# Class 3's routing ahead of class 2's gates, and the first 32 tiles multiplied in SBUF

## The chip, the cores and the metric

The kernel runs on one core of a Trainium2 chip. TensorE (PE) multiplies matrices, VectorE (DVE) and ScalarE (ACT) work element by element, GpSimd (POOL) issues the gathers, SyncE (SP) issues the plain loads and stores. The metric is the device time of one execution in microseconds.

## The reference

One encoder block for 512 tokens of width 1024, in float32. The token-mixing half ends in a residual `x`. The channel-mixing half, which this case is about, is a product-key retrieval layer:

```
h = rmsnorm(x) ;  q = (h @ w_q) in 8 heads x 2 halves of 128
s = q . sub_keys                    # 128 scores for each head and half
top_s, top_i = top_k(s, 16)         # 16 of 128, each half
best_s, best_j = top_k(all 256 sums of a pair, 16)
expert = i0 * 128 + i1 ;  gate = softmax(best_s)     # 8 x 16 = 128 of 16384 experts a token
act = gelu(u_tab[expert] . h) * gate
x = x + sum(act * v_tab[expert]) ;  out = rmsnorm(x)
```

`u_tab` and `v_tab` are 16384 x 1024 each, 67 MB each.

## The kernel before

The 512 tokens are four classes of 128 (class r holds the tokens t with t mod 4 = r). Classes 0 and 3 are *gathered*: for each of a token's 128 experts one row of `u` and one of `v` is fetched by an indirect DMA (`row_of`, L237, 128 rows of 4 KB for 128 tokens, 0.52 MB), and DVE multiplies and sums (L261, L344). Classes 1 and 2 (`ND` = 2, together 256 columns, `TD`) are done *densely*: all 16384 experts, in 128 tiles of 128, are multiplied on PE, and a dense matrix of gates, zero but for the 128 chosen experts of each token, is multiplied in.

**Order.** Class 0's front half comes first, exactly, then that of classes 1 to 3 together. Meanwhile class 0's gathers run as `steps` (L118): a generator that yields after each gathered row. `gather_steps` (L124) is called at fixed places of the stream of work, adds an estimated duration times `rate`, and takes that many steps; so the gathers are spread by estimates, not by need. Class 0 has 256 steps (`NA`), class 3 has 261 (`NCL`): four of routing, 128 rows of `u`, 128 of `v` and the end. By the code some 215 of the 517 are taken before the early tiles; each early tile takes 4.5 x 0.38 = 1.71. The rest is spread evenly over the main loop (L811).

**Routing** (`route`, L175) is DVE work only: the two top-16 searches and the pick of the expert numbers for two heads; four calls make a class. Classes 1 and 2 are routed at L696 to L710, in the pool `l2`. Class 3's scores go to DRAM (`s_dram`, L712) and come back in `gathered` (L322), which is class 3's generator, at L327 to L332: it routes, casts the numbers to `eidx` (L335), and goes on to the rows.

**Gates** (`gates`, L748) of class r: PE transposes expert numbers and gates; DVE writes two one-hots for eight tokens at a time (`hot`, L768), ACT scales one of them (L771), PE multiplies them to gates of 128 x 128 experts for each token (`pg`, L776), ACT copies these to `stg` (L779), and one DMA for each 32 tokens writes `stg` to `g_dram` (L780). Both classes' gates are issued by L797 to L804 with the same priority, class 1's, then class 2's routing, then class 2's gates.

**Early tiles** (`early`, L784). For 28 pairs of tiles the up-projection is done ahead: tiles of `ut` are loaded (0.52 MB each, four buffers `rawp`), multiplied in plain float32 by `h2T` (L742, `mm`), and go through gelu (L743). The first 20 pairs stay in SBUF (`KEPT`, the tile `pre`), the other eight go to DRAM (`SPILLED`, `a_dram`). `G0` and `G1` hold two of the pairs behind the transposes of class 1's and class 2's gates on PE.

**Main loop** (L827). Every 8 tiles two loads bring the gates of both classes (`gl`, L831). For a pair of tiles the activations are there (kept), loaded (spilled), or computed (`up_pair` with `h2S`, split in two float32r halves, three products). Then the activations are multiplied by the gates (L849), split, and multiplied with the split tile of `v` into `acc` (L861). At the end `finish` (L221) normalises and writes.

SP, DVE, ACT, PE and POOL each work through one list in order; the lists are laid out when the kernel is built, by priorities and estimated durations.

Of the kernel before, what the change touches and what calls it, by code (L numbers as in the profile page):

```python
# [9 lines left out]
F32 = mybir.dt.float32  # L10
# [4 lines left out]
ALU = mybir.AluOpType  # L15
# [4 lines left out]
P = 128  # L20
# [8 lines left out]
NC = 50  # L29
ND = 2  # L30
TD = ND * P
NB = 4 * ND

NPRE = 40
NSP = 16
KEPT = list(range(0, NPRE, 2))
SPILLED = list(range(NPRE, NPRE + NSP, 2))

# [1 line left out]
GB = 16  # L40
# [9 lines left out]
VUS = 2.75  # L50

G0 = 3
G1 = 12
LATE = 15.0


def body(ctx, tc, a, out):
    nc = tc.nc
# [63 lines left out]
    taken = 0  # L122
# [120 lines left out]
    def in_row(name, k, n):  # L243
        row = gp.tile([P, D], F32, tag="row", name=name, bufs=GPB)
        return row[:, 0:k * n].rearrange("p (k n) -> p k n", k=k)
# [4 lines left out]
    def routed():  # L250
        return [gp.tile([P, 8, 16], F32, tag=t, name=t + "_g") for t in ("bv", "ef")]
# [70 lines left out]
    def gathered(r, behind):  # L322

        h2g = gp.tile([P, D], F32, tag="h2g", name="h2g")
        nc.sync.dma_start(h2g, h2_dram)
        bv, ef = routed()
        for c in range(4):  # L327
            sg = in_row("sg", 4, P)
            nc.sync.dma_start(sg, s_dram[c])
            for _ in route(gp, sg, bv[:, 2 * c:2 * c + 2, :], ef[:, 2 * c:2 * c + 2, :], row_eq):  # L330
                pass
            yield  # L332
        eidx = gp.tile([P, P], I32, tag="eidx", name="eidx")
        gate = gp.tile([P, P], F32, tag="gate", name="gate")
        nc.vector.tensor_copy(eidx, ef.rearrange("p h k -> p (h k)"))  # L335
        softmax16(bv, gate)
        xg = load_x(r)
        pend = []

        def down():  # L340
            k0, act = pend.pop(0)
            for k in range(GB):
                row = row_of(a["v"], eidx[:, k0 + k:k0 + k + 1])
                nc.vector.scalar_tensor_tensor(xg, row, act[:, k:k + 1], xg, op0=ALU.mult, op1=ALU.add)  # L344
                yield

        for k0 in range(0, P, GB):
            ab = gp.tile([P, GB], F32, tag="abk", name="ab", bufs=2)
            yield from u_rows(eidx, h2g, ab, k0, GB)
            if k0 == 0:  # L350
                behind()
            act = gp.tile([P, GB], F32, tag="act", name="act", bufs=3)
            nc.scalar.activation(act, ab, AF.Gelu)
            nc.vector.tensor_tensor(act, act, gate[:, k0:k0 + GB], ALU.mult)
            if pend:
                yield from down()
            pend.append((k0, act))
        yield from down()
        finish(gp, r, xg)
        yield  # L360


    NA, NCL = 256, 261
    gp = pool(ctx, "gp", 1, side="right", reuse_waits="tile")

    ph = ExitStack()
# [3 lines left out]
    with ExitStack() as p1:  # L370
# [317 lines left out]
        late = []  # L688
        gs_ = [l2.tile([P, P], F32, name=f"g{r}") for r in range(ND)]

        def gate_of(r):
            sums.append(softmax16(bvs[r], gs_[r]))
# [3 lines left out]
        def route_now(j, c, ssb):  # L696
            for _ in route(l2, ssb, bvs[j][:, 2 * c:2 * c + 2, :], efs[j][:, 2 * c:2 * c + 2, :],
                           lambda: l2.tile([P, 16, NC], F32, tag="eq", name="eq")):
                pass
# [48 lines left out]
    def gates(r, ef, g):  # L748
        e = l2.tile([P, P], I32, tag="e", name="e", bufs=1)
        nc.vector.tensor_copy(e, ef.rearrange("p h k -> p (h k)"))  # L750
        ij = l2.tile([P, 2, P], I32, tag="ij", name="ij", bufs=1)
        nc.vector.tensor_scalar(ij[:, 0, :], e, 7, None, op0=ALU.logical_shift_right)
        nc.vector.tensor_scalar(ij[:, 1, :], e, 127, None, op0=ALU.bitwise_and)
        ijf = l2.tile([P, 2, P], F32, tag="ijf", name="ijf", bufs=1)
        nc.vector.tensor_copy(ijf, ij)
        t = ppg.tile([P, 4, P], F32, tag="pg", name="tr")
        for k, src in enumerate((ijf[:, 0, :], ijf[:, 1, :], g)):
            tr = nc.tensor.transpose(t[:, k, :], src, ident)
        trs.append(tr)
        tt = l2.tile([P, 3, P], F32, tag="tt", name="tt")  # L760
        nc.scalar.copy(tt, t[:, 0:3, :])
        for blk in range(4):
            stg = gb.tile([P, P, 32], F32, tag="stg", name="stg")
            for b8 in range(4):
                c0 = blk * 32 + b8 * 8
                hot = [gb.tile([P, 8, P], F32, tag=f"hot{k}", name="hot") for k in range(2)]
                for k in range(2):
                    nc.vector.tensor_tensor(hot[k], iota.unsqueeze(1).to_broadcast([P, 8, P]),  # L768
                                            tt[:, k, c0:c0 + 8].unsqueeze(2).to_broadcast([P, 8, P]), ALU.is_equal)
                for m in range(8):  # L770
                    nc.scalar.activation(hot[0][:, m, :], hot[0][:, m, :], AF.Copy,  # L771
                                         scale=tt[:, 2, c0 + m:c0 + m + 1])
                for q in range(2):
                    ps = ppg.tile([P, 4, P], F32, tag="pg", name="pg")
                    for m in range(4):
                        nc.tensor.matmul(ps[:, m, :], hot[1][:, 4 * q + m, :], hot[0][:, 4 * q + m, :],  # L776
                                         start=True, stop=True)
                    c1 = b8 * 8 + 4 * q
                    nc.scalar.copy(stg[:, :, c1:c1 + 4].rearrange("p i c -> p c i"), ps)  # L779
            nc.sync.dma_start(g_dram[r][blk], stg)  # L780

    npre = len(KEPT) + len(SPILLED)
    rate = PRE
    def early(n, behind=None):  # L784
        i = (KEPT + SPILLED)[n]
        if n < len(KEPT):
            up_pair(i, lambda k: pre[:, 2 * n + k, :], PUS, behind=behind)
            return
        ges = [gep.tile([P, TD], F32, tag="ge", name="ges") for _ in range(2)]
        up_pair(i, lambda k: ges[k], PUS, behind=behind)  # L790
        for k in range(2):
            nc.sync.dma_start(a_dram[2 * (n - len(KEPT)) + k], ges[k])

    trs = []
    for n in range(G0):
        early(n)
    with tc.high_priority(offset=1500):  # L797
        for r in range(ND):
            gates(r, efs[r], gs_[r])
            if r == 0:  # L800
                with tc.issue_after(sums[0].ins):
                    for args in late:
                        route_now(*args)
                gate_of(1)  # L804
    for n in range(G0, npre):
        early(n, trs[0] if n == G0 else trs[1] if n == G1 else None)
    pr_.close()
    assert taken > NA + 5 + GB
    pva.close()
    pacc = pool(ctx, "pacc", 1, space=PSUM, reuse_waits="tile")  # L810
    rate = (NA + NCL - taken) / ((P - 2 * npre) * UUS + P * VUS - LATE)  # L811
# [15 lines left out]
    for i in range(0, P, 2):  # L827
        if i % 8 == 0:
            gl = glp.tile([P, NB, 8, 32], F32, tag="gl", name="gl")
            for r in range(ND):  # L830
                nc.sync.dma_start(gl[:, 4 * r:4 * r + 4, :, :],  # L831
                                  g_dram[r][:, :, i:i + 8, :].rearrange("b j i c -> j b i c"))
        if i in KEPT:
            ge = [pre[:, i + k, :] for k in range(2)]
        else:
            ge = [gep.tile([P, TD], F32, tag="ge", name="ge") for _ in range(2)]
            if i in SPILLED:
                for k in range(2):
                    nc.sync.dma_start(ge[k], a_dram[2 * SPILLED.index(i) + k])
            else:  # L840
                up_pair(i, lambda k: ge[k], UUS, h2S)
        ops = []
        for k in range(2):
            g3 = ge[k].rearrange("p (b c) -> p b c", c=32)
            raw = load(vt, i + k)
            vh = hip.tile([P, D], F32R, tag="hi", name="vh")
            vl = lop.tile([P, D], F32R, tag="lo", name="vl")
            split(vh, vl, raw)
            nc.vector.tensor_tensor(g3, g3, gl[:, :, (i + k) % 8, :], ALU.mult)  # L849
            ah = ep.tile([P, TD], F32R, tag="ah", name="ah")  # L850
            al = ep.tile([P, TD], F32R, tag="al", name="al")
            last = split(ah, al, ge[k])
            ops.append(([ah, al], [vh, vl]))
            gather_steps(VUS, last)
        order = [(k, t, q) for k in range(2) for t in range(ND) for q in range(2)]
        if i == P - 2:
            order = [(k, t, q) for t in range(ND) for q in range(2) for k in range(2)]
        for k, t, q in order:
            c = slice(t * P, t * P + P)
            f = slice(q * 512, q * 512 + 512)  # L860
            mm(acc[t][:, f], [x[:, c] for x in ops[k][0]], [x[:, f] for x in ops[k][1]], False, i + k == P - 1)  # L861
# [75 lines left out]
```

## Time and profile before

| | us |
|---|---|
| median of 3 runs (1809.59 to 1811.98) | 1809.87 |
| the profiled execution | 1802.23 |
| its span, first to last instruction | 1800.5 |
| PE busy | 1623.4 (90%) |
| DVE busy | 1324.7 (74%) |
| ACT busy | 714.4 (40%) |
| POOL busy | 691.9 (38%) |

548.53 MB were moved, 305 GB/s over the span. Early tiles begin at 813 us, the main loop's first tile of `v` is issued at 1116 us, and its first computed pair ends its up-projection at 1342 us.

The rows below come from several views of one profiled execution. Times are in us from the span's start, durations of one instruction in ns where marked. A busy time is the union of the instructions' spans, with their number behind it (x). The DMA share is the mean busy share of the core's 16 DMA engines. In square brackets stands the idle time of the engine before an instruction, and what ended it.

### The profile page before, as it was taken

Reading aid. Unit: us, or ns where it says so; the run is one execution under the profiler, and the core shown is the slowest. Engines: PE = TensorE matmul, PEld = TensorE weight load, DVE = VectorE, ACT = ScalarE, POOL = GpSimd, SP = SyncE. Lnnn points to the kernel's source line nnn. Section 1 sums busy time; section 2 is a strip of 40 time slices with the busy share of each in tenths; the row PEclk is TensorE's granted clock in tenths of the full one; section 3 lists DMA queues with packets and bytes.
Section 4 is the critical chain, followed back from the end, with each engine's and each line's share of the span. In section 5 each row is a group of like instructions: output and inputs, shape, how many; then the busy total and the mean of one; then the engine's idle time right before and its main releaser. Section 6 shows DMA issues by size and latency. Waiting matters only on the chain.

```text
span 1800.5 us, 25509 instructions
## 1 busy us (share of the span) xinstructions
PE 1623.4 (90%) x9184; PEld 1379.4 (77%) x9184; DVE 1324.7 (74%) x2818; ACT 714.4 (40%) x1264; POOL 691.9 (38%) x535
## 2 busy tenths in 40 slices
PE   7999987899689997999999967778989999999997
PEld 6988867777489874887878956556768887888886
DVE  3332119899999344589957966899989888888895
ACT  4324211344443323224777711233444443444443
POOL 0000000277776443333430044566545454444440
PEclk9999999898899998999999988799999999999999
DMA  5335776499999899777885599999999999999994
GB/s 198 94 108 154 262 259 212 159 366 354 315 331 355 308 358 363 272 292 265 306 318 203 213 392 401 362 396 380 363 392 373 354 380 356 374 365 358 372 353 148
DMA packets 164335, 548.53 MB, mean 305 GB/s; under 512 B 17008, under 2 KB 37488, under 8 KB 163056
## 3 DMA queue, kind: packets, MB, share of 16 engines
q1 hardware_dynamic: 90480, 278.43, 43.3%
q0 software_dynamic: 73728, 268.47, 39.6%
q8 instruction: 72, 1.18, 0.3%
q14 instruction: 55, 0.45, 0.1%
HBM read 522.19 MB, written 24.64 MB: 304 GB/s over the span
## 4 chain that ended last, share of the span: by engine, by line
PE 58%; DVE 20%; DMA 10%; issue 6%; ACT 4%; POOL 2%; DVEq 0%; SPq 0%; POOLq 0%; ACTq 0%
PE pj L112 7%; PE pj L114 6%; PE pj L116 6%; PE pj L115 6%; PE pu_t L112 5%; DVE row L261 5%; PE acc L115 5%; PE acc L116 4%; PE acc L114 4%; DMA raw<-in_ut_dram 4%; DVE vl L90 3%; PE acc_A L295 3%; DMA row<-in_u_dram,eidx 2%; PE pg L776 2%; PE pu_t L116 2%
## 5 line engine op out<-in xcount | busy, mean ns | idle before, releaser
L239 POOL DMA_INDIRECT row<-in_u_dram,eidx x256 | 357.0, 1394 | 407.5 <-DVE eidx L335 98.8
L261 DVE SCALAR_TENSOR_TENSOR row<-row,h2g 128x1024 f32<-128x1024 f32 x256 | 308.4, 1222 | 9.6 <-DMA row<-in_u_dram,eidx 9.3
L239 POOL DMA_INDIRECT row<-in_v_dram,eidx x128 | 181.2, 1415 | 169.8 <-DVE xg L344 82.5
L115 PE MATMUL acc<-vl,ah 128*128 128x512 f32 x512 | 208.3, 416 | 33.7 <-DVE vl L90 33.5
L239 POOL DMA_INDIRECT row<-in_v_dram,eT x128 | 143.9, 1125 | 223.9 <-PE acc_A L295 175.8
L112 PE MATMUL pu_t<-h2T,raw 128*128 128x256 f32 x896 | 207.6, 388 | 21.7 <-DMA raw<-in_ut_dram 21.7
L112 PEld LDWEIGHTS pu_t<-h2T,raw 128*128 128x128 f32 x896 | 171.0, 195 | 53.6 <-issue 26.2
L114 PE MATMUL acc<-vh,ah 128*128 128x512 f32 x512 | 192.1, 408 | 17.4 <-ACT vh L89 15.4
L90 DVE TENSOR_TENSOR wlo<-raw,whi 128x1024 fp32r<-128x1024 f32 x88 | 107.7, 1223 | 130.3 <-ACT whi L89 130.3
L116 PE MATMUL acc<-vh,al 128*128 128x512 f32 x512 | 199.5, 406 | 0.3 <-DVE al L90 0.3
L89 ACT CAST whi<-raw 128x1024 fp32r<-128x1024 f32 x88 | 92.1, 1048 | 248.3 <-PE pj L115 174.4
L90 DVE TENSOR_TENSOR vl<-raw,vh 128x1024 fp32r<-128x1024 f32 x128 | 155.6, 1222 | 23.8 <-ACT vh L89 23.5
L114 PE MATMUL pu_t<-h2S_hi,uhi 128*128 128x256 f32 x576 | 165.0, 286 | 5.6 <-ACT uhi L89 4.5
L116 PE MATMUL pu_t<-h2S_hi,ulo 128*128 128x256 f32 x576 | 165.1, 287 | 3.9 <-DVE ulo L90 3.8
L344 DVE SCALAR_TENSOR_TENSOR xg<-row,act,xg 128x1024 f32<-128x1024 f32 x128 | 164.1, 1282 | 0.6
L115 PE MATMUL pu_t<-h2S_lo,uhi 128*128 128x256 f32 x576 | 164.3, 285 | 0.0
L115 PEld LDWEIGHTS acc<-vl,ah 128*128 128x128 f32 x512 | 99.9, 195 | 72.9 <-DVE vl L90 52.4
L89 ACT CAST vh<-raw 128x1024 fp32r<-128x1024 f32 x128 | 133.0, 1045 | 31.5 <-DMA raw<-in_v_dram 21.8
L114 PEld LDWEIGHTS acc<-vh,ah 128*128 128x128 f32 x512 | 96.6, 195 | 44.9 <-ACT vh L89 22.7
L151 POOL TENSOR_TENSOR rs<-ms,mhalf 128x1 f32<-128x1 f32 x16 | 9.0, 562 | 298.8 <-DVE ms L149 298.7
L114 PEld LDWEIGHTS pu_t<-h2S_hi,uhi 128*128 128x128 f32 x576 | 111.3, 193 | 10.8 <-ACT uhi L89 7.2
L116 PE MATMUL pj<-hT_hi,wlo 128*128 128x384 f32 (+1 forms) x320 | 101.1, 356 | 19.5 <-DVE wlo L90 19.5
(241 smaller groups left out, 3387.7 us busy)
## 6 DMA issues: line engine op xcount, KB each, us to landing
raw<-in_ut_dram SPq DMA_DIRECT2D x128, 512.0 KB, 6.7
raw<-in_v_dram SPq DMA_DIRECT2D x128, 512.0 KB, 6.6
raw<-in_w_in_dram SPq DMA_DIRECT2D x88, 512.0 KB, 4.4
raw<-in_wq_dram SPq DMA_DIRECT2D x32, 512.0 KB, 4.5
g_dram<-stg SPq DMA_DIRECT2D x8, 2048.0 KB, 7.8
gl<-g_dram SPq DMA_DIRECT2D x32, 512.0 KB, 9.3
raw<-in_wa_dram SPq DMA_DIRECT2D x16, 512.0 KB, 6.1
raw<-in_wo_dram SPq DMA_DIRECT2D x16, 512.0 KB, 4.8
```

What stands on the lines that cost most here:

```text
L89: nc.scalar.copy(hi, src)
L90: return nc.vector.tensor_tensor(lo, src, hi.bitcast(F32), ALU.subtract)
L112: on_pe = nc.tensor.matmul(ps, l[0], r[0], start=first, stop=last)
L114: nc.tensor.matmul(ps, l[0], r[0], start=first, stop=False)
L115: nc.tensor.matmul(ps, l[0], r[1], start=False, stop=False)
L116: on_pe = nc.tensor.matmul(ps, l[1], r[0], start=False, stop=last)
L151: nc.gpsimd.tensor_tensor(rs, ms, mhalf, ALU.pow)
L239: nc.gpsimd.indirect_dma_start(out=row, out_offset=None, in_=table, in_offset=bass.IndirectOffsetOnAxis(ap=at, axis=0))
L261: nc.vector.scalar_tensor_tensor(row, row, 1.0, h2g, op0=ALU.mult, op1=ALU.mult, accum_out=ab[:, k:k + 1])
L295: last = nc.tensor.matmul(ps[32 * j:32 * j + 32, c], ex[:, j, :], rows[j][:, c], start=n == 0, stop=n == 31)
L344: nc.vector.scalar_tensor_tensor(xg, row, act[:, k:k + 1], xg, op0=ALU.mult, op1=ALU.add)
L776: nc.tensor.matmul(ps[:, m, :], hot[1][:, 4 * q + m, :], hot[0][:, 4 * q + m, :], start=True, stop=True)
```

## The change

Class 3's routing leaves the generator. A new function `route_last` does it in the pool `l2`, with the loads of its scores into the buffers of class 2's scores, and is issued with the gates' priority behind class 1's gates and class 2's routing. `gathered` takes the result from `found` and begins with `eidx`; its steps are 257.

Class 2's gates are issued later, ahead of early pair 16 of the list, when tiles 0 to 31 of `pre` have been issued. For each block of 32 tokens `pre` of these 32 tiles is multiplied by `stg` in SBUF, and only tiles 32 to 127 are written to `g_dram`. In the main loop the first 32 tiles load and multiply class 1's gates alone. `NSP` goes from 16 to 30: 15 pairs are spilled, so 35 pairs are early. `G1` goes from 12 to 19.

```diff
--- before.py
+++ after.py
@@ -32,7 +32,7 @@
 NB = 4 * ND
 
 NPRE = 40
-NSP = 16
+NSP = 30
 KEPT = list(range(0, NPRE, 2))
 SPILLED = list(range(NPRE, NPRE + NSP, 2))
 
@@ -50,7 +50,9 @@
 VUS = 2.75
 
 G0 = 3
-G1 = 12
+G1 = 19
+
+NG2 = 32
 LATE = 15.0
 
 
@@ -323,13 +325,7 @@
 
         h2g = gp.tile([P, D], F32, tag="h2g", name="h2g")
         nc.sync.dma_start(h2g, h2_dram)
-        bv, ef = routed()
-        for c in range(4):
-            sg = in_row("sg", 4, P)
-            nc.sync.dma_start(sg, s_dram[c])
-            for _ in route(gp, sg, bv[:, 2 * c:2 * c + 2, :], ef[:, 2 * c:2 * c + 2, :], row_eq):
-                pass
-            yield
+        bv, ef = found[r]
         eidx = gp.tile([P, P], I32, tag="eidx", name="eidx")
         gate = gp.tile([P, P], F32, tag="gate", name="gate")
         nc.vector.tensor_copy(eidx, ef.rearrange("p h k -> p (h k)"))
@@ -360,7 +356,8 @@
         yield
 
 
-    NA, NCL = 256, 261
+    NA, NCL = 256, 257
+    found = {}
     gp = pool(ctx, "gp", 1, side="right", reuse_waits="tile")
 
     ph = ExitStack()
@@ -777,7 +774,11 @@
                                          start=True, stop=True)
                     c1 = b8 * 8 + 4 * q
                     nc.scalar.copy(stg[:, :, c1:c1 + 4].rearrange("p i c -> p c i"), ps)
-            nc.sync.dma_start(g_dram[r][blk], stg)
+            m = NG2 if r else 0
+            if m:
+                c0 = P + blk * 32
+                nc.vector.tensor_tensor(pre[:, 0:m, c0:c0 + 32], pre[:, 0:m, c0:c0 + 32], stg[:, 0:m, :], ALU.mult)
+            nc.sync.dma_start(g_dram[r][blk][:, m:, :], stg[:, m:, :])
 
     npre = len(KEPT) + len(SPILLED)
     rate = PRE
@@ -791,21 +792,33 @@
         for k in range(2):
             nc.sync.dma_start(a_dram[2 * (n - len(KEPT)) + k], ges[k])
 
+    def route_last():
+
+        found[3] = bv, ef = routed()
+        for c in range(4):
+            ssb = l2.tile([P, 4, P], F32, tag="ssb1", name="ssb", bufs=4)
+            nc.sync.dma_start(ssb, s_dram[c])
+            for _ in route(l2, ssb, bv[:, 2 * c:2 * c + 2, :], ef[:, 2 * c:2 * c + 2, :],
+                           lambda: l2.tile([P, 16, NC], F32, tag="eq", name="eq")):
+                pass
+
     trs = []
     for n in range(G0):
         early(n)
     with tc.high_priority(offset=1500):
-        for r in range(ND):
-            gates(r, efs[r], gs_[r])
-            if r == 0:
-                with tc.issue_after(sums[0].ins):
-                    for args in late:
-                        route_now(*args)
-                gate_of(1)
+        gates(0, efs[0], gs_[0])
+        with tc.issue_after(sums[0].ins):
+            for args in late:
+                route_now(*args)
+        gate_of(1)
+        route_last()
     for n in range(G0, npre):
+        if 2 * n == NG2:
+            with tc.high_priority(offset=1500):
+                gates(1, efs[1], gs_[1])
         early(n, trs[0] if n == G0 else trs[1] if n == G1 else None)
     pr_.close()
-    assert taken > NA + 5 + GB
+    assert taken > NA + GB
     pva.close()
     pacc = pool(ctx, "pacc", 1, space=PSUM, reuse_waits="tile")
     rate = (NA + NCL - taken) / ((P - 2 * npre) * UUS + P * VUS - LATE)
@@ -827,7 +840,7 @@
     for i in range(0, P, 2):
         if i % 8 == 0:
             gl = glp.tile([P, NB, 8, 32], F32, tag="gl", name="gl")
-            for r in range(ND):
+            for r in range(1 if i < NG2 else ND):
                 nc.sync.dma_start(gl[:, 4 * r:4 * r + 4, :, :],
                                   g_dram[r][:, :, i:i + 8, :].rearrange("b j i c -> j b i c"))
         if i in KEPT:
@@ -846,7 +859,8 @@
             vh = hip.tile([P, D], F32R, tag="hi", name="vh")
             vl = lop.tile([P, D], F32R, tag="lo", name="vl")
             split(vh, vl, raw)
-            nc.vector.tensor_tensor(g3, g3, gl[:, :, (i + k) % 8, :], ALU.mult)
+            nb = 4 if i < NG2 else NB
+            nc.vector.tensor_tensor(g3[:, 0:nb], g3[:, 0:nb], gl[:, 0:nb, (i + k) % 8, :], ALU.mult)
             ah = ep.tile([P, TD], F32R, tag="ah", name="ah")
             al = ep.tile([P, TD], F32R, tag="al", name="al")
             last = split(ah, al, ge[k])
```

## Rows read from the trace of the kernel before

**Rows 1.** Windows by stage: us; PE, PEld, DVE, ACT, POOL busy; clock; DMA; GB/s.

```profile
980.00:1044.00 64.00, 64.00 (x372) 58.41 (x371) 63.17 (x235) 47.03 (x103) 0.00 (x0) 1.00 0.60 212
1044.00:1120.00 76.00, 54.28 (x222) 45.87 (x221) 46.23 (x96) 7.27 (x21) 36.36 (x29) 0.87 1.05 401
1120.00:1339.00 219.00, 181.88 (x680) 133.19 (x679) 195.06 (x259) 78.80 (x116) 125.34 (x89) 0.92 0.99 377
1339.00:1755.00 416.00, 390.87 (x2396) 343.80 (x2395) 368.01 (x474) 179.20 (x268) 197.37 (x139) 0.99 0.98 367
1755.00:1800.50 45.50, 32.64 (x201) 28.57 (x199) 27.13 (x40) 17.95 (x34) 1.79 (x3) 0.93 0.45 149
```

**Rows 2.** The page, the chain that ended last, by engine.

```profile
PE 58%; DVE 20%; DMA 10%; issue 6%; ACT 4%; POOL 2%; DVEq 0%; SPq 0%; POOLq 0%; ACTq 0%
```

**Rows 3.** Timeline of POOL: start, us, instruction, idle before and its releaser.

```profile
1044.32 2.25 POOL L239 DMA_INDIRECT row<-in_u_dram,eidx  x1 [98.76 <-DVE eidx L335]
```

**Rows 4.** Timeline of DVE.

```profile
916.33 0.98 DVE L209 TENSOR_REDUCE ef<-eq 128x16 f32<-128x800 f32 x1
937.52 1.23 DVE L768 TENSOR_TENSOR hot<-iota,tt 128x1024 f32<-128x1024 f32 x1 [7.64 <-ACT tt L761]
...
1043.34 0.22 DVE L335 CAST eidx<-ef_g 128x128 int32<-128x128 f32 x1
```

**Rows 5.** Windows over class 3's routing: DVE alone, then instructions on `hot` alone.

```profile
960.80:1043.50 82.70, 81.42 (x309) 1.00 0.59 210
...
960.80:1043.50 82.70, 25.32 (x208) 25.27 (x208) 25.93 (x23) 28.36 (x94) 1.00 0.59 210
```

**Rows 6.** Groups by line: busy us, mean ns, idle before.

```profile
L768 DVE TENSOR_TENSOR hot<-iota,tt 128x1024 f32<-128x1024 f32 x64 | 75.1, 1218 | 20.4 <-ACT tt L761 7.6 <-issue 7.4 <-PE pg L776 5.3
...
L849 DVE TENSOR_TENSOR ge<-ge,gl 128x256 f32<-128x256 f32 x88 | 37.1, 422 | 22.9 <-ACT ge L743 20.4 <-DMA ge<-a_dram 2.5
```

**Rows 7.** Chain of waits, in order of time, 1010 to 1026 us.

```profile
1016.36 3.89 PE pu_t L112 x18
1020.24 1.78 PE pg L776 x16
```

**Rows 8.** DMA issues: count, KB each, us to landing.

```profile
g_dram<-stg SPq DMA_DIRECT2D x8, 2048.0 KB, 7.8
gl<-g_dram SPq DMA_DIRECT2D x32, 512.0 KB, 9.3
...
a_dram<-ges SPq DMA_DIRECT2D x16, 128.0 KB, 12.5
```

**Rows 9.** Timeline of PE, last stage.

```profile
1602.64 0.39 PE L116 MATMUL acc<-vh,al 128*128 128x512 f32 x1
1602.87 0.28 PE L114 MATMUL pu_t<-h2S_hi,uhi 128*128 128x256 f32 x1
...
1608.61 0.39 PE L114 MATMUL acc<-vh,ah 128*128 128x512 f32 x1
```

**Rows 10.** DMA issues, 917 to 980 us, then 980 to 1120.

```profile
raw<-in_ut_dram SPq DMA_DIRECT2D x10, 512.0 KB, 6.0
...
raw<-in_ut_dram SPq DMA_DIRECT2D x24, 512.0 KB, 8.1
...
row<-in_u_dram,eidx POOLq DMA_INDIRECT x28, 10.4
```

**Rows 11.** Instructions on `pu_t` (min/median/max ns, first, last start); window 937 to 1036.5.

```profile
L743 ACT ACTIVATE ge<-pu_t x72: 376/384/387, 1342.3 to 1782.9; 128x256 f32<-128x256 f32 x72
...
L743 ACT ACTIVATE ges<-pu_t x16: 365/383/384, 1041.0 to 1119.9; 128x256 f32<-128x256 f32 x16
...
937.00:1036.50 99.50, 66.95 (x298) 55.02 (x297) 6.88 (x19) 1.00 0.62 227
```

**Rows 12.** DMA issues, 1120 to 1339 us.

```profile
row<-in_v_dram,eidx POOLq DMA_INDIRECT x48, 7.2
row<-in_u_dram,eidx POOLq DMA_INDIRECT x41, 7.2
```

## The prediction

> **What bounds the kernel now.** I read the stage table first [rows 1]. From 1044 us to 1755 us the DMA engines are busy 1.05, 0.99 and 0.98 of the time at 401, 377 and 367 GB/s; no other engine is that full in all three stages (PE 0.71, 0.83, 0.94; DVE 0.61, 0.89, 0.88). Just before, from 980 to 1044, PE is busy all of 64 us at full clock, but the DMA engines are only 0.60 busy at 212 GB/s, and POOL issues nothing. The chain that ended last [rows 2] gives PE 58% and DMA only 10%; that is an average in which each short step on PE, released by a transfer just landed, counts as PE, so I take the limit of each stage from the stage table. POOL's timeline names what keeps it idle: the first gather of a class 3 row starts at 1044.32, after 98.76 us of waiting for `eidx` [rows 3], the last product of class 3's routing. DVE's timeline shows why that is late: class 2's routing is over at 916.33, the one-hots of class 2's gates take DVE from 937.52, class 3's routing goes on between them, and `eidx` is written at 1043.34 [rows 4].
>
> So the reading is: as soon as class 3's gathers run, transfers set the pace to the end; before that PE does, while the DMA engines wait for work. The time is then the start of the gathers, plus the bytes that are left at that point over the DMA rate, plus a tail.
>
> **Routing of class 3 ahead of class 2's gates.** Its DVE work does not change, it moves. From its first instruction at 960.8 to 1043.5 DVE is busy 81.42 us, of which the one-hots take 25.93 [rows 5]; 55.5 us is left for the routing. In the changed kernel it follows class 2's routing on DVE, which ends at 917.3 (916.33 plus 0.98). Two pairs of one-hots of class 1's gates are still to come there, at 1.22 us each [rows 6] 4.9 us. 917.3 + 55.5 + 4.9 and a microsecond for the softmax is 979. The four loads of scores go on SP's queue earlier, 256 KB each; `ssb` has four buffers that class 2's routing frees one by one before 917, so I cost their wait at nothing (if one blocked SP, weight tiles up to four ahead are in `rawp` as cover). The gathers start at 979 instead of 1044.3, 65 us earlier. Queued behind the routing on DVE are class 2's one-hots, and behind them ACT's scaling and PE's `pg`; that is what the move of the gates is for, below.
>
> In those 65 us the kernel before moved 13.8 MB (212 GB/s). From 1044 to 1755 it moved 76 x 401 + 219 x 377 + 416 x 367 = 265.7 MB in 711 us, 374 GB/s. At that rate 13.8 MB take 37 us: 28 us of DMA time is won. This is the main term.
>
> **What the stretch from 917 to 979 loses or wins.** Class 2's gates leave it: one write of 2 MB (2.10 MB), and seven blocks of eight tokens, which PE works off at one per 3.89 + 1.78 us with 1.78 us of `pg` each [rows 7], 13 us. PE fills these with up-projections: 18 matmuls take 3.89 us, so a pair of tiles (32) takes 6.9 us, and 13 us hold 3.7 tiles of 0.524 MB, 1.9 MB. Bytes out and bytes in cancel: 0.
>
> **Class 2's gates later, and the product in SBUF.** Four writes lose 32 of 128 tiles, 4 x 0.52 MB, and four of the 32 loads of `gl` go, 4 x 0.52 MB [rows 8]: -4.2 MB. The four added products on DVE (128x1024, strided in runs of 32) have no row of their own; nearest are the one-hot of the same size at 1.22 us [rows 6] and the 256-element product at 0.42 us, 1.7 us for 1024 elements. So 5 to 7 us, against 32 products of the main loop that halve (0.42 towards 0.2 us, 6 us back): 0 on a DVE that is 0.88 busy. SP's write of the rest now waits for this product; behind it on SP stand weight loads, covered as above.
>
> **Seven more spilled pairs.** 14 writes and 14 loads of 128 KB more [rows 8], +3.7 MB; with the above -0.5 MB, 1.4 us at 374 GB/s. On PE a pair costs 6.9 us early, but in the main loop 48 matmuls from 1602.87 to 1608.61, 5.74 us [rows 9]: 7 x 1.2 = +8 us of PE. What hides it: after 979 PE has some 18.5 pairs (128 us; counted under the slower rival), 16 blocks of gates (28 us), 29 pairs of 5.74 (166 us) and 64 pairs of 24 `acc` matmuls at 0.233 (358 us; 0.23 is the pitch in [rows 9]), in sum 680 us, where the forecast has some 780. If that cover were gone, 8 us are lost. DVE loses 14 splits of the one-hot's size, ACT as many casts; neither sets the end. The gathers themselves are the same 256 rows; 28 more of them are issued in the first stage (70 tiles of 1.71 steps instead of 56, and four steps of routing less), which fills the DMA engines but moves no byte to another total.
>
> **The sum.** -28 (idle DMA time filled) - 1.4 (bytes) + 0 + 0 = -29 us. The profiled execution took 1802.23 us at a span of 1800.5; it becomes 1773. The median shown, 1809.87, lies 7.6 us above the profiled execution, so I take the difference from that: 1781 us.
>
> **Bounds of what no row shows.** When `eidx` is ready: at the earliest 972, if the one-hots fall behind the routing (-3 us more), at the latest with DVE's order as interleaved as before: then 55.5 us of routing stretches to the 82.7 us that it took among one-hots and ends at 1006, and 27 us x 0.43 of idle DMA time, 12 us, is lost again. I take 979, the sum of the routing's own rows. The rate afterwards: from 367 GB/s, the last stage's, up to the 401 of [rows 1]. I take 374, the mean. At 367 throughout, the 279 MB left take 14 us more; if the last stage, with seven up-projections fewer, runs at the 377 of the stage before it, 152.7 MB take 11 us less.
>
> **Rivals.**
> *More is won, 1765 us.* The last stage is not bound by DMA alone: PE is 0.94 and DVE 0.88 busy there. With seven pairs fewer it runs nearer to the DMA engines' pace: -11 us by the line above, and -3 to -5 us from an earlier `eidx`: -45. For it: the rate of 401 GB/s, seen where PE and DVE have slack. Against: 0.98 busy DMA engines at 367.
>
> *Little is won, 1797 us.* The routing stays interleaved and ends at 1006 (-28 + 12), and the gathers, which now share DVE with the one-hots of class 2, wait there in order. For it: in 1044 to 1120 DVE was only 0.61 busy and still POOL issued only 28 rows in 76 us [rows 10]. Against: there the DMA engines were 1.05 busy, so the rows were late for the transfers, not for DVE.
>
> *Slower, 1829 us: spilled pairs at the pace of today.* The sixteen spilled tiles end at 1041.0 to 1119.9 [rows 11], 10.5 us a pair, with PE 0.71 busy, while gathers and weight loads share the DMA engines. Now class 2's gates would run from 979 to 1076 (97 us, as from 937.52 to 1034.5). Beside them 9.5 pairs were done [rows 11]; so 10.5 of the 20 kept pairs were done by 937, 42 us at 6.9 us make 16.5 by 979, 26 are done by 1076, and nine at 10.5 us end the first stage at 1171 instead of 1120. The next 35 pairs at today's 219 / 28 = 7.8 us end at 1445. Today it is 461.5 us from 1339 to the end; seven pairs fewer at 12.4 us (71 steps of one tile from 1342.3 to 1782.9 [rows 11]) leave 375: 1820, +19 us. It decides from where the spilled pairs and the first 35 of the main loop keep these paces. For it: the landing of a weight tile grows from 6.0 us to 8.1 us once the gathers run [rows 10], and a late tile holds up all that stands behind it in PE's program. Against: the old 7.8 us held 89 gathered rows in 28 pairs [rows 12], 3.2 each, and rows that were issued earlier are not there to slow it; the whole would move 280 MB from 979 on at 352 GB/s, below every stage after 1044.
>
> A rule bears on this rival. The Trainium skill, "DMA: Bandwidth & Descriptors", section "Queues, rings and completion order", says that each DMA engine takes turns between the queues that have work, a packet at a time, so POOL's gathers could not take more than about half from SP's loads. By that rule a spilled pair (two tiles of weights, its writes and a share of `gl`, some 1.6 MB) at half of 401 GB/s would take 8 us, the nine pairs 22 us less, and this rival would end near 1807 instead of 1829. The longer landing in [rows 10] agrees in direction; the pace of 10.5 us is slower than the rule has it, so I keep 1829.
>
> **How the numbers follow.** Forecast 0.50 (its own range 1770 to 1792), more won 0.13, little won 0.15, slower 0.22. The range for 8 in 10 goes from 1757 (the gain of -45 and 8 us beyond it) to 1814, which leaves out the upper half of the slower case. A measurement of this kernel can tell about 0.2%, 3.6 us, from no change. Faster: 0.50 + 0.13 and 0.09 of the third case, 0.72. Within 0.2%: 0.04 of the third and 0.04 of the slower case, 0.08. Slower: 0.18 of the slower case and 0.02 of the third, 0.20.
>
> **What would show it.** POOL's first class 3 row near 979, and no wait of 98 us for `eidx` (some 35 us stay, from 945). DMA share near 1.0 from there on, not from 1044. The first matmul of `acc` between 1130 and 1165, the last stage shorter by some 80 us. Four `gl` loads fewer, `g_dram` writes of two sizes. The forecast is wrong if `eidx` comes after 1010, if the DMA rate after the start of the gathers falls under 365 GB/s, or if PE stands still between 980 and 1080 for one-hots that are queued on DVE behind rows not yet landed.

## The result and the profile after

The changed kernel takes 1786.54 us (median of 4 runs, 1783.36 to 1789.98) where the kernel before takes 1809.73 us on the same chip (1803.83 to 1811.98): ratio 0.9873, 95% interval 0.9847 to 0.9899, 23 us faster (18 to 28). The profiled execution took 1787.65 us at a span of 1785.9, against 1802.23 and 1800.5: the two traces show 15 us of the 23, because the profiled execution of before is faster than any of its timed runs, and that of after lies at its median. What follows explains the 15 us that can be seen.

The stage table of the changed kernel, with the columns of [rows 1], cut where its stages change:

```profile
980.00:1006.60 26.60, 25.60 (x148) 22.73 (x148) 25.95 (x65) 21.99 (x54) 0.00 (x0) 1.00 0.52 173
1006.60:1044.00 37.40, 35.37 (x205) 31.24 (x205) 31.49 (x43) 23.36 (x53) 27.57 (x20) 1.00 0.97 377
1044.00:1120.00 76.00, 56.50 (x245) 47.97 (x243) 52.24 (x99) 15.16 (x36) 39.45 (x33) 0.91 1.03 405
1120.00:1202.00 82.00, 64.45 (x263) 53.17 (x264) 45.53 (x54) 5.85 (x16) 47.00 (x38) 0.90 0.98 381
1202.00:1423.00 221.00, 208.20 (x843) 155.42 (x842) 198.50 (x276) 98.32 (x143) 106.91 (x68) 0.98 1.00 378
1423.00:1740.00 317.00, 305.12 (x1890) 269.48 (x1889) 282.11 (x360) 140.67 (x211) 146.07 (x101) 0.99 0.97 365
1740.00:1785.90 45.90, 33.02 (x201) 28.66 (x200) 26.25 (x39) 17.45 (x34) 1.65 (x3) 0.93 0.44 140
```

The picture is that of [rows 1], shifted. From 1006.6 us on the DMA engines are full. Up to 1740 they move 37.4 x 377 + 76 x 405 + 82 x 381 + 221 x 378 + 317 x 365 = 275.3 MB in 733.4 us, 375 GB/s; before it was 374. The tail is 45.9 us, before 45.5. So what changed is when the full stretch begins. POOL's timeline has the last gather of class 0 and the first of class 3, which answers to [rows 3]:

```profile
950.96 0.94 POOL L241 DMA_INDIRECT row<-in_v_dram,eT  x1 [0.31 <-PE pg L773]
1006.61 1.82 POOL L241 DMA_INDIRECT row<-in_u_dram,eidx  x1 [54.71 <-PE pu_t L114]
```

Class 3's gathers start at 1006.61 instead of 1044.32. That is 37.7 us earlier, not the 65 that I had forecast. DVE's timeline says why (compare [rows 4]); class 2's routing ends at 922.1, and `eidx` comes at 1005.62:

```profile
921.15 0.98 DVE L211 TENSOR_REDUCE ef<-eq 128x16 f32<-128x800 f32 x1
...
956.50 2.35 DVE L765 TENSOR_TENSOR hot<-iota,tt 128x1024 f32<-128x1024 f32 x2
...
1005.62 0.23 DVE L331 CAST eidx<-ef_g 128x128 int32<-128x128 f32 x1
```

Between the two DVE is busy 83.35 of 83.5 us. Two windows, DVE alone, and below it the instructions on `hot` (their DVE time is the third of the busy columns: PE, PEld, DVE, ACT):

```profile
922.10:1005.60 83.50, 83.35 (x297) 1.00 0.67 243
```

```profile
922.10:1005.60 83.50, 23.60 (x192) 23.18 (x192) 30.39 (x26) 31.67 (x105) 1.00 0.67 243
```

Of 83.35 us the one-hots take 30.39, 26 of them. Four are those of class 1's gates that I had counted; the other 22, from 946.35 us on, are class 2's. The rest, 53 us, is the routing, as worked out (55.5). Class 2's gates did not wait for it: their transposes are on PE at 942.31, six microseconds after those of the kernel before (936.44):

```profile
942.31 0.38 PE L755 MATMUL tr<-ident,ijf 128*128 128x128 f32 x2
```

The change gives both the same raised priority (`offset=1500`), and class 2's gates start 20 us after class 2's routing. In DVE's list, which was laid out when the kernel was built, pairs of one-hots stand between the pieces of class 3's routing.

### The profile page after: what moved, and what is told of

Read it like the earlier page. It is cut to its first block, busy times and chain, and to the rows that moved or that the text cites. A ratio compares the mean times of both kernels' runs of the same rounds, so it can differ in the third digit from the quotient of the medians.

```text
span 1785.9 us, 25387 instructions
## 1 busy us (share of the span) xinstructions
PE 1625.6 (91%) x9072; PEld 1374.4 (77%) x9072; DVE 1309.0 (73%) x2808; ACT 699.8 (39%) x1250; POOL 696.1 (39%) x535
## 4 chain that ended last, share of the span: by engine, by line
PE 60%; DVE 16%; DMA 12%; issue 5%; ACT 3%; POOL 1%; another core or an unknown queue 1%; ACTq 0%; SPq 0%; DVEq 0%; POOLq 0%
PE pj L114 7%; PE pj L116 6%; PE pu_t L114 6%; PE pj L118 6%; PE pj L117 6%; DMA raw<-in_ut_dram 6%; DVE row L263 5%; PE acc L117 4%; PE acc L118 4%; PE acc L116 4%; PE acc_A L297 3%; DMA raw<-in_v_dram 2%; PE pu_t L118 2%; DVE hot L765 2%; PE pu_t L116 2%
## 5 line engine op out<-in xcount | busy, mean ns | idle before, releaser
L114 PE MATMUL pu_t<-h2T,raw 128*128 128x256 f32 x1120 | 262.1, 391 | 36.6 <-DMA raw<-in_ut_dram 33.6
L114 PEld LDWEIGHTS pu_t<-h2T,raw 128*128 128x128 f32 x1120 | 215.4, 196 | 79.3 <-issue 41.6
L117 PE MATMUL acc<-vl,ah 128*128 128x512 f32 x512 | 203.5, 407 | 10.6 <-DVE vl L92 10.4
L116 PE MATMUL acc<-vh,ah 128*128 128x512 f32 x512 | 188.2, 401 | 11.2 <-ACT vh L91 7.4
L118 PE MATMUL acc<-vh,al 128*128 128x512 f32 x512 | 195.1, 397 | 0.0
L116 PE MATMUL pu_t<-h2S_hi,uhi 128*128 128x256 f32 x464 | 132.4, 285 | 2.7 <-ACT uhi L91 2.7
L118 PE MATMUL pu_t<-h2S_hi,ulo 128*128 128x256 f32 x464 | 132.4, 285 | 1.9 <-DVE ulo L92 1.9
L117 PE MATMUL pu_t<-h2S_lo,uhi 128*128 128x256 f32 x464 | 131.8, 284 | 0.0
L116 PE MATMUL pj<-hT_hi,whi 128*128 128x384 f32 (+1 forms) x320 | 114.1, 357 | 6.6 <-ACT u L544 3.3
```

The source lines that it names most:

```text
L114: on_pe = nc.tensor.matmul(ps, l[0], r[0], start=first, stop=last)
L116: nc.tensor.matmul(ps, l[0], r[0], start=first, stop=False)
L117: nc.tensor.matmul(ps, l[0], r[1], start=False, stop=False)
L118: on_pe = nc.tensor.matmul(ps, l[1], r[0], start=False, stop=last)
```

## The experiments

The theory (T): once class 3's gathers run, the rest takes its bytes over some 375 GB/s, so the time follows the start of the gathers. The rival (R): the gain comes from the seven pairs of up-projections that left the last stage, where PE is nearly full. The ratios of the experiments are to the kernel before on the same chip, with its median at 1804 to 1805 us there. An idle share is the part of a stretch in which the DMA engines could have moved more: 60% busy is an idle share of 0.4.

**The order on DVE, enforced.** The changed kernel with this edit:

```diff
-            nc.vector.tensor_reduce(ef[:, h, :], eq, axis=AX.X, op=ALU.add)
+            routed_at[0] = nc.vector.tensor_reduce(ef[:, h, :], eq, axis=AX.X, op=ALU.add)
...
         route_last()
+        held = routed_at[0]
...
-            with tc.high_priority(offset=1500):
+            with tc.high_priority(offset=1500), tc.issue_after(held.ins):
                 gates(1, efs[1], gs_[1])
```

`held` is the last instruction of class 3's routing; `issue_after` puts the DVE instructions of class 2's gates behind it.

> The changed kernel, with DVE's work of class 2's gates held behind the last instruction of class 3's routing. Theory T (transfers set the pace as soon as class 3's gathers run, at some 375 GB/s, and before that the DMA engines are half idle): the first gather comes near 980 us instead of 1006.6, and of these 27 us the idle share of 0.48 is won, 12 us: 1774 us. Rival R (the gain comes from the seven pairs of up-projections that left the last stage, where PE is 0.94 busy): the order on DVE is no matter, 1783 to 1790 us. A third view: class 2's gates, now late, hold up PE, and it is slower than 1790.

Measured: 1771.11 us (1769.55 to 1783.33, 6 runs), 0.9836 (0.9799 to 0.9873), span 1768.1. POOL's first row of class 3, then the stages:

```profile
977.22 0.94 POOL L243 DMA_INDIRECT row<-in_u_dram,eidx  x1 [29.72 <-DVE ijf L754]
```

```profile
984.00:1044.00 60.00, 55.56 (x329) 49.58 (x328) 56.95 (x80) 47.68 (x124) 42.85 (x25) 1.00 0.98 378
1044.00:1200.00 156.00, 122.06 (x568) 102.95 (x567) 102.74 (x150) 42.42 (x92) 76.98 (x61) 0.90 1.03 403
1200.00:1420.00 220.00, 214.13 (x923) 164.65 (x922) 205.17 (x286) 99.64 (x147) 114.59 (x72) 0.98 0.99 373
1420.00:1725.00 305.00, 289.28 (x1796) 254.46 (x1795) 270.50 (x343) 137.44 (x205) 145.35 (x96) 1.00 0.97 363
```

The gathers start at 977.22, where the prediction had 979, and the span is 17.8 us shorter than that of the changed kernel, for a start 29.4 us earlier; T had 12. Against the kernel before, 0.0164 of 1805 us is 30 us (23 to 36), where the prediction had 29. Against the changed kernel it is less certain: by the two ratios the order is worth 0.0037, 7 us, and their intervals overlap. The run below without the seven pairs, whose gathers start with those of the changed kernel, was timed on the same chip: its six runs took 1779.34 to 1787.75 us and have a mean 8.6 us above that of the six here, of which four took 1769.55 to 1771.71 and two 1780.24 and 1783.33. So an earlier start on its own is a gain, near T's 12 us, which R did not have. That class 2's gates come later does not show: PE is idle more between 984 and 1200, but the DMA engines are not.

**The routing alone.** The kernel before with `route_last` and `found` of the change, and neither the product nor the seven pairs:

```diff
                 gate_of(1)
+                route_last()
     for n in range(G0, npre):
```

The rest of the edit is `route_last` itself and `gathered` beginning with `eidx`, as in the change.

> The kernel before, with class 3's routing ahead of class 2's gates and nothing else: 16 spilled tiles, all gates of class 2 by way of DRAM. T: gathers start near 1006 instead of 1044, 38 us at an idle share of 0.43: 16 us faster than before, some 1793 us, with the DMA engines full from there on. R: no pair has left the last stage, so within 4 us of before, 1806 to 1814.

Measured: 1789.38 us (1784.82 to 1797.0, 7 runs), 0.9926 (0.9896 to 0.9956), span 1786.4: 13 us (8 to 19), where T had 16. First row of class 3, and the full stretch:

```profile
1002.94 1.18 POOL L239 DMA_INDIRECT row<-in_u_dram,eidx  x1 [53.73 <-issue]
```

```profile
1008.00:1755.00 747.00, 669.62 (x3608) 565.05 (x3607) 633.61 (x851) 298.17 (x470) 370.49 (x253) 0.96 0.98 370
```

Moving the routing alone brings the gathers forward by 41 us and brings more than half of the gain; R had none.

**The seven pairs alone.** The kernel before with `NSP = 30`:

```diff
-NSP = 16
+NSP = 30
```

> The kernel before with 30 spilled tiles instead of 16 and nothing else. T: the gathers start where they did, and 3.7 MB more are moved; no gain, 1806 to 1820 us. R: the seven pairs leave the last stage, and most of the changed kernel's 23 us are there: 1785 to 1795 us.

Measured: 1804.89 us (1795.59 to 1814.18, 12 runs), 0.9989 (0.9963 to 1.0015). The gathers start where they did, and nothing is won:

```profile
1046.79 2.25 POOL L239 DMA_INDIRECT row<-in_u_dram,eidx  x1 [98.76 <-DVE eidx L335]
```

R fails. But nothing is lost either; the time is just under T's range, 2 us faster (7 faster to 3 slower): the 3.7 MB more that T has to move would be 10 us at 375 GB/s. The full stretch runs at 377 GB/s where the kernel before had 374:

```profile
1044.00:1755.00 711.00, 632.22 (x3162) 518.54 (x3161) 593.70 (x815) 252.26 (x391) 355.05 (x257) 0.96 0.99 377
```

**The change without the seven pairs.** The changed kernel with `NSP = 16`:

```diff
-NSP = 30
+NSP = 16
```

> The changed kernel with 16 spilled tiles instead of 30. T: the start of the gathers stays at 1006 and 3.7 MB go away: 1776 to 1788 us. R: the gain goes with the seven pairs, 1803 us or more.

Measured: 1782.62 us (1779.34 to 1787.75, 6 runs), 0.9873 (0.9844 to 0.9903), span 1786.0: the same as the changed kernel. Its gathers start at 1006.55. The 3.7 MB that it moves less are not seen in the time: after 1006 it runs at 370 GB/s where the changed kernel had 375.

```profile
1006.00:1740.00 734.00, 664.27 (x3551) 560.57 (x3552) 623.15 (x842) 297.04 (x473) 375.91 (x257) 0.96 0.98 370
```

With the run of the pairs alone, R falls: the seven pairs are worth nothing, either way round. T is not borne out whole: in both runs the bytes of the pairs cost no time, and the rate is higher with them (377 against 374, 375 against 370). That PE, relieved of seven pairs in the last stage, lets the transfers run faster there would fit; no run separates it.

**Fewer bytes.** The changed kernel, with the gates loaded for every second group of eight tiles; the tiles of the other groups are multiplied by the gates of the group before, so the output is not the reference's:

```diff
-        if i % 8 == 0:
+        if i % 16 == 0:
             gl = glp.tile([P, NB, 8, 32], F32, tag="gl", name="gl")
```

> The changed kernel with the gates loaded only for every second group of eight tiles (14 loads of 512 KB fewer in the main loop; the groups between use the gates of the group before, so the output differs). Theory T (after the gathers have started the time is bytes over 375 GB/s): 7.3 MB fewer, 20 us: 0.976 of the kernel before, some 15 to 20 us under the changed kernel. Rival R (in the last stage PE and DVE, 0.96 and 0.89 busy, set the pace): within 5 us of the changed kernel.

Measured: 1759.83 us (1756.74 to 1768.31, 5 runs), 0.9755 (0.9736 to 0.9774): 0.0118 under the changed kernel, 21 us (15 to 27) for 7.3 MB, where 375 GB/s make 20; R had at most 5. The gathers start at 1010.67, 4 us later than in the changed kernel. The stretch from 1006 on at 376 GB/s:

```profile
1006.00:1720.00 714.00, 665.75 (x3452) 558.57 (x3453) 612.91 (x835) 285.87 (x467) 376.96 (x257) 0.97 0.99 376
```

PE does the same work there as in the changed kernel, in 20 us less. Here what is taken from the transfers comes off the time one to one. That fewer waits for `gl` did part of it was not tested apart; the rate, unchanged at 376, speaks for the bytes.

**The product alone.** The kernel before with class 2's gates at early pair 16, the product in SBUF and the shorter `gl` loads, `G1` at 19; routing and spilled pairs as before:

```diff
+                nc.vector.tensor_tensor(pre[:, 0:m, c0:c0 + 32], pre[:, 0:m, c0:c0 + 32], stg[:, 0:m, :], ALU.mult)
-            nc.sync.dma_start(g_dram[r][blk], stg)
+            nc.sync.dma_start(g_dram[r][blk][:, m:, :], stg[:, m:, :])
```

> The kernel before with class 2's gates after early pair 16 and multiplied in SBUF for the first 32 tiles, with nothing else of the change. T: the gathers start where they did, near 1044 us; 4.2 MB fewer to move, 11 us at most: 1794 to 1806 on a chip where the kernel before takes 1805. If class 2's gates come later than before and class 3's routing with them less interleaved, the gathers start some us earlier and it is at the lower end. R: no change, as no pair leaves the last stage.

Measured: 1801.05 us (1795.48 to 1804.82, 12 runs), 0.9977 (0.9956 to 0.9999), 4 us (0 to 8). The bytes that go are 4.2 MB, 11 us; the gathers start 8 us later than before, which at the old idle share of 0.4 takes some 3 us back. The 8 us that this leaves are the upper end of what was measured:

```profile
1052.39 2.98 POOL L240 DMA_INDIRECT row<-in_u_dram,eidx  x1 [103.56 <-DVE eidx L336]
```

Routing, product and pairs alone make 0.9926 x 0.9977 x 0.9989 = 0.9892, the whole change 0.9873 (0.9847 to 0.9899): the parts add up within their intervals.

**Class 3's routing ahead of class 2's routing too.** The changed kernel with two lines changed:

```diff
-            ssb = l2.tile([P, 4, P], F32, tag="ssb1", name="ssb", bufs=4)
+            ssb = l2.tile([P, 4, P], F32, tag="ssb0", name="ssb", bufs=2)
...
         with tc.issue_after(sums[0].ins):
+            route_last()
             for args in late:
                 route_now(*args)
         gate_of(1)
-        route_last()
```

> The changed kernel with class 3's routing ahead of class 2's routing too. T: class 3's numbers are ready near 920 to 935 us, the gathers can follow class 0's last row near 951, and the DMA idle time from there to 1006 (shares of 0.39 to 0.52) is won: 25 to 30 us under the changed kernel, 1756 to 1762 us, or 0.972 of before. Rival: class 2's gates now come after some 980 us and share DVE with the gathered rows, PE waits for them, and the gain of an earlier start is lost: not faster than with class 2's gates held back, 0.9836 of before.

Measured: 1768.18 us (1765.91 to 1772.5, 5 runs), 0.981 (0.979 to 0.983), by its median the fastest version that computes the reference. Its first row of class 3 and some of its stages:

```profile
958.79 0.94 POOL L241 DMA_INDIRECT row<-in_u_dram,eidx  x1 [12.16 <-DVE bp L168]
```

```profile
960.00:980.00 20.00, 20.00 (x96) 17.54 (x93) 16.53 (x54) 3.58 (x7) 16.31 (x13) 1.00 0.94 358
980.00:1000.00 20.00, 13.14 (x49) 10.76 (x48) 19.88 (x51) 3.14 (x6) 8.99 (x8) 0.74 1.01 407
1000.00:1020.00 20.00, 20.00 (x111) 18.04 (x110) 18.37 (x29) 14.89 (x43) 9.65 (x7) 1.00 0.87 302
1020.00:1040.00 20.00, 20.00 (x123) 18.40 (x123) 17.14 (x26) 12.87 (x30) 16.84 (x11) 1.00 0.94 352
...
1180.00:1220.00 40.00, 37.98 (x156) 28.65 (x156) 27.52 (x42) 15.04 (x22) 12.17 (x9) 1.00 0.90 305
1220.00:1300.00 80.00, 80.00 (x343) 62.00 (x342) 76.62 (x98) 39.10 (x59) 46.41 (x28) 1.00 0.98 367
...
1400.00:1720.00 320.00, 307.57 (x1914) 271.80 (x1913) 288.23 (x368) 145.35 (x215) 154.42 (x103) 1.00 0.99 369
```

The gathers start at 958.79, 48 us earlier than in the changed kernel, but the span is only 19.5 us shorter (1766.4), and no shorter beyond the noise than with the enforced order, which starts 18 us later. T's forecast, 1756 to 1762 us, failed, and the rival's, not faster than with class 2's gates held back, came true within the noise. Two things are visible. The routing was over at 924.3, as T had it, but `eidx`, which only casts its result, stands further down in DVE's list, among class 2's routing. POOL had ended class 0's rows at 946.6 and waited 12 us for it:

```profile
923.29 0.98 DVE L211 TENSOR_REDUCE ef_g<-eq 128x16 f32<-128x800 f32 x1
...
957.82 0.21 DVE L331 CAST eidx<-ef_g 128x128 int32<-128x128 f32 x1
```

And the head start was used up in the first stage. How many rows it takes is tied to its tiles (1.71 steps each), not to the start: 88 rows of class 3 in the changed kernel, with the enforced order and here. The gelu of its last spilled tile starts at 1187.8 with the enforced order and at 1189.7 here. The bytes moved between 958.8 and 1190, with the enforced order and then here, are nearly the same:

```profile
DMA packets 29711, 86.64 MB, mean 375 GB/s; under 512 B 2864, under 2 KB 11696, under 8 KB 29184
DMA packets 29840, 87.10 MB, mean 377 GB/s; under 512 B 2880, under 2 KB 11712, under 8 KB 29313
```

What the earlier start moved sooner is given back where the DMA share falls: 0.87 and 0.94 from 1000 to 1040, when the one-hots of class 2's gates, late now, share DVE with the rows, and 0.90 from 1180 to 1220. Which of these sets the end of the first stage no run shows.

**More gathers in the first stage.** The version above with

```diff
-PRE = 0.38
+PRE = 0.55
```

> As the one before, and the early tiles take 4.5 x 0.55 steps of gathering instead of 4.5 x 0.38, so that class 3's rows do not run out in the first stage (in the changed kernel the DMA share falls to 0.76 and 0.89 near 1170 to 1190 us). T: what is idle there is 4 to 5 us, won on top: 0.970 of before. Rival: class 0's rows, which come first, are taken closer together where PE is full, and the early stage gets longer: slower than the one before by 5 us or more.

Measured: 1796.17 us (1792.98 to 1802.51, 12 runs), 0.9958 (0.9939 to 0.9976), 28 us slower than the version above, although class 3's gathers start at 928.75, the earliest of all:

```profile
928.75 0.94 POOL L241 DMA_INDIRECT row<-in_u_dram,eidx  x1 [12.70 <-issue]
```

```profile
1220.00:1300.00 80.00, 60.89 (x220) 45.87 (x220) 69.58 (x93) 25.06 (x38) 45.75 (x35) 0.87 0.96 356
1300.00:1400.00 100.00, 97.58 (x407) 75.64 (x405) 84.58 (x118) 45.85 (x70) 38.54 (x24) 0.98 0.89 322
1400.00:1720.00 320.00, 316.95 (x1909) 279.41 (x1908) 266.52 (x348) 152.04 (x225) 113.44 (x77) 1.00 0.95 342
```

This is where T ends: its forecast, 0.970, failed, and the rival's, slower by 5 us or more, came true. The first stage takes 114 rows of class 3 instead of 88. It ends 9 us later than in the version above (last gelu of a spilled tile at 1198.7 instead of 1189.7), and the stored pairs behind it are held up more: from 1220 to 1300 PE is busy 61 of 80 us, in the version above 80, while the DMA engines are as full, and the first gelu of the last stage comes at 1453.6 instead of 1409.3. With more rows taken early, fewer are left for the main loop; from 1300 on the DMA share is 0.89 and then 0.95 at 322 and 342 GB/s, and from 1400 on PE is busy 317 of 320 us. So PE waits first and sets the pace later, with the DMA engines waiting then. A start of the gathers is worth its idle time only as long as rows are left to fill the rest.

## Why the prediction was right, point by point

*Transfers set the pace from the first gather of class 3.* Right in the main: the rate after the start is 374, 375 and 376 GB/s in the kernel before, the changed one and the one with fewer bytes, and 7.3 MB less are 21 us less. But it is not fixed: 370 in the two runs that move the routing and keep sixteen spilled tiles, where 5 GB/s over 734 us are 10 us. And its limit, which the prediction did not have, is the last two experiments.

*The routing ends at 979.* Wrong; this is the term that was mis-sized. The step was "it follows class 2's routing on DVE", with two pairs of one-hots in between. The amount of routing was right (53 us for 55.5), but 26 one-hots came in between, not four, since class 2's gates start as early as before. The bound in the prediction for an interleaved order was 1006, and it was 1005.62. With the order enforced the gathers started at 977.22, and the gain was 30 us (23 to 36) for the 29 forecast: the sum fits the order that I had assumed, and the kernel has the other one. By the prediction's own price the late start costs 12 us, which makes 1793 us; that 1786.5 was measured, 5.5 us from the forecast, is in part luck. In the trace that the forecast is made from it was worth 15 us, near the 16 of the rival "little is won", which had this start; the timed medians differ by 23, between the two.

*Bytes out and in cancel from 917 on.* Nearly. One window from 917 to 1006.6 us in the trace of the kernel before, and the same in that of the changed one:

```profile
917.00:1006.60 89.60, 89.60 (x548) 75.33 (x547) 62.82 (x184) 68.00 (x160) 10.56 (x12) 1.00 0.70 254
```

```profile
917.00:1006.60 89.60, 88.55 (x533) 71.55 (x533) 88.88 (x313) 68.02 (x160) 14.79 (x12) 1.00 0.66 241
```

254 and 241 GB/s over 89.6 us are 22.8 and 21.6 MB: 1.2 MB, 3 us, were lost there.

*The product in SBUF costs DVE nothing on the path.* Right. Four products at 1.22 us make 5 us, and the halved products of the main loop at 0.28 us (not 0.2) give 4.5 back, not 6. In groups by line:

```profile
L863 DVE TENSOR_TENSOR pre<-pre,gl 128x128 f32<-128x128 f32 x32 | 6.8, 282 | 13.3 <-DMA gl<-g_dram 11.2 <-issue 2.1
...
L780 DVE TENSOR_TENSOR pre<-pre,stg 128x1024 f32<-128x1024 f32 x4 | 4.8, 1218 | 1.1 <-ACT stg L776 0.6 <-ACT pre L740 0.5
```

*Seven more pairs cost 8 us of PE, hidden, and 3.7 MB.* Right in sum: alone they change nothing, and taken out they change nothing. The bytes, 10 us at the prediction's 374 GB/s, do not show in either run. In the prediction they stood against the 4.2 MB of the product, 11 us, of which 4 (0 to 8) were measured. That the two cancel came out; neither size did.

*The slower rival* was half right. The rows of gelu by `pu_t`, which answer to [rows 11]:

```profile
L740 ACT ACTIVATE ge<-pu_t x58: 372/383/387, 1426.1 to 1768.1; 128x256 f32<-128x256 f32 x58
...
L740 ACT ACTIVATE ges<-pu_t x30: 383/383/385, 1054.6 to 1202.3; 128x256 f32<-128x256 f32 x30
```

The spilled tiles end at 1054.6 to 1202.3, 10.2 us a pair, as it had it (10.5), and the first stage ends at 1202; the first matmul of `acc` comes at 1207.6, not between 1130 and 1165 as in "What would show it". Its next step failed: the following 35 pairs took 221 us (1202 to 1423), 6.3 us a pair, not 7.8. They held 68 gathered rows, 1.9 a pair, where 28 pairs had held 89 before, 3.2 each; more rows had gone with the spilled pairs, as the prediction's "against" had it. The last stage took 363 us instead of 461.5: the first stage's delay was given back there. Late pairs in one stage were no loss here while the DMA engines stayed full.

## What to carry to other kernels

Where transfers fill the second half of a kernel, look for the first instant at which they can, and what that waits for: here one routing on DVE, and the idle DMA share of the stretch before it (0.4 to 0.5) is about what each microsecond was worth, down to a start at 977 us. Beyond that an earlier start won nothing clear, since the number of gathered rows that the stage takes was fixed by its tiles. A priority was not an order here: two pieces of work at the same priority interleaved once the second was ready, so work out when the second becomes ready, and put in an edge if the order is what counts. And moving work between stages that are paced by the same transfers was worth nothing by itself.

## What was not expected

In the changed kernel POOL stops for 20 us in the full stretch, and the DMA share falls:

```profile
1158.25 0.93 POOL L241 DMA_INDIRECT row<-in_v_dram,eidx  x1 [0.61 <-DVE xg L340]
1179.70 1.86 POOL L241 DMA_INDIRECT row<-in_v_dram,eidx  x1 [20.52 <-DVE xg L340]
```

```profile
1160.00:1170.00 10.00, 10.00 (x48) 8.61 (x47) 0.00 (x0) 1.15 (x3) 0.00 (x0) 1.00 1.03 417
1170.00:1180.00 10.00, 10.00 (x48) 8.68 (x47) 1.91 (x3) 1.25 (x4) 0.30 (x1) 1.00 0.76 235
1180.00:1190.00 10.00, 10.00 (x48) 8.80 (x47) 9.74 (x8) 1.15 (x3) 7.86 (x8) 1.00 0.89 316
```

POOL waits for DVE's `xg`, DVE for a small gelu of 16 columns on ACT (L349, 0.21 us), and this one stands in ACT's list behind six gelus of spilled tiles. The first of them waits 17 us for PE, which itself stood still for 11.96 us until a weight tile landed; the others follow at PE's pace, one per 3.5 us:

```profile
1154.57 9.75 PE L114 MATMUL pu_t<-h2T,raw 128*128 128x256 f32 x36 [11.96 <-DMA raw<-in_ut_dram]
...
1160.09 0.38 ACT L740 ACTIVATE ges<-pu_t 128x256 f32<-128x256 f32 x1 [17.00 <-PE pu_t L114]
...
1177.81 0.21 ACT L349 ACTIVATE act<-ab 128x16 f32<-128x16 f32 x1
```

So a late weight tile, and the place of the small gelu in ACT's list, held up the gathers by way of three lists in order. By the shares it cost some 3 to 4 us of DMA time (0.24 and 0.11 of 10 us each), an estimate; no run took it away.
